# FiLM layer on one core: projections loaded as 16 partitions of four rows, contraction as four accumulated matmuls, compute in program order

## The chip, the cores and the metric

The kernel runs on one core of one Trainium2 chip. The metric is device time in microseconds (us). The times come on two levels: of the 29 runs of the kernel before in this study, 21 lie between 84.39 and 84.72 us and eight between 85.83 and 86.6. Runs more than 1.5% above the fastest of their kernel are marked slow.

## The reference, cut to what matters

```python
# x: (32, 512, 256) f32, conditioning: (32, 64), gamma_proj and beta_proj: (64, 256)
gamma = conditioning @ gamma_proj
beta = conditioning @ beta_proj
return x * (1 + gamma[:, None, :]) + beta[:, None, :]
```

A FiLM layer scales and shifts x by factors (gamma, beta) that a small input, the conditioning, sets. 16.78 MB come in, 16.78 MB go out, and each element gets one multiply and one add. The two small products (32 x 64 by 64 x 256) are all the arithmetic that TensorE has.

## The kernel before: the parts that the argument touches

x is treated as four slabs of eight batches; each slab gives every partition 32 rows of 256. All loads of x go out on SyncE's queue ahead of the compute (slab 0 in two parts, so five loads; four are issued in the first 3 us, the last at 10.3 us). The small inputs and all stores go out on ScalarE's queue. gamma and beta come out of TensorE already repeated onto the 128 partitions, because the conditioning matrix is transposed and repeated by a matmul against a repeated identity.

```python
nc.scalar.dma_start(out=cond_s, in_=conditioning)
gbproj = consts.tile([cond_dim, 2 * dim], f32)          # 64 partitions
nc.scalar.dma_start(out=gbproj[:, :dim], in_=gamma_proj)
nc.scalar.dma_start(out=gbproj[:, dim:], in_=beta_proj)
# ... loads of x on nc.sync, transposed and repeated conditioning in cond_T ...
for s in range(SLABS):
    nc.tensor.matmul(p_t, lhsT=cond_T[:, s * P : (s + 1) * P], rhs=gbproj, start=True, stop=True)
    nc.scalar.activation(out=s_t[:, :dim], in_=p_t[:, :dim], func=Identity, bias=1.0, scale=1.0)
    nc.scalar.copy(out=s_t[:, dim:], in_=p_t[:, dim:])
# ...
for s in range(SLABS):
    for r0 in range(0, ROWS, GROUP):                     # 2 pieces of 16 rows a slab
        # 11 rows on VectorE, 5 on GpSimd
        nc.vector.scalar_tensor_tensor(out=v, in0=rows(g_p, nv), scalar=1.0, in1=v, op0=ALU.add, op1=ALU.mult)
        nc.gpsimd.tensor_tensor(out=w, in0=w, in1=rows(g_s, nw), op=ALU.mult)
        nc.vector.tensor_add(out=v, in0=v, in1=rows(b_p, nv))
        nc.gpsimd.tensor_tensor(out=w, in0=w, in1=rows(b_s, nw), op=ALU.add)
        nc.scalar.dma_start(out=o_v[s, :, r0 : r0 + GROUP, :], in_=xs[:, r0 : r0 + GROUP, :])
```

Of the kernel before, what the change touches and what calls it, by code (L numbers as in the profile page):

```python
# [2 lines left out]

# [5 lines left out]


@with_exitstack
def kernel(
    ctx: ExitStack,
    tc: tile.TileContext,
    x: bass.AP,
    conditioning: bass.AP,
    gamma_proj: bass.AP,
    beta_proj: bass.AP,
    out: bass.AP,  # L20
):
    nc = tc.nc
    f32 = mybir.dt.float32
    ALU = mybir.AluOpType

    batch, seq, dim = x.shape
    cond_dim = conditioning.shape[1]
    P = 128
    SLABS = 4
    BS = batch // SLABS  # L30
    REP = P // BS
    ROWS = BS * seq // P
    assert SLABS * BS == batch and REP * BS == P and ROWS * REP == seq

    x_v = x.flatten_outer_dims().rearrange("(s p r) d -> s p r d", s=SLABS, p=P)
    o_v = out.flatten_outer_dims().rearrange("(s p r) d -> s p r d", s=SLABS, p=P)

    LOADS = {0: [8, 24]}
    GROUP = 16
    ON_DVE = 11  # L40

    consts = ctx.enter_context(tc.tile_pool(name="consts", bufs=1))
    xpool = ctx.enter_context(tc.tile_pool(name="xpool", bufs=1))
    psum = ctx.enter_context(tc.tile_pool(name="psum", bufs=1, space=bass.MemoryType.PSUM))


    cond_s = consts.tile([batch, cond_dim], f32)
    nc.scalar.dma_start(out=cond_s, in_=conditioning)  # L48
    gbproj = consts.tile([cond_dim, 2 * dim], f32)
    nc.scalar.dma_start(out=gbproj[:, :dim], in_=gamma_proj)  # L50
    nc.scalar.dma_start(out=gbproj[:, dim:], in_=beta_proj)

    slabs = []
    for s in range(SLABS):
        xs = xpool.tile([P, ROWS, dim], f32, name=f"xs{s}")
        slabs.append(xs)
        r = 0
        for n in LOADS.get(s, [ROWS]):
            nc.sync.dma_start(out=xs[:, r : r + n, :], in_=x_v[s, :, r : r + n, :])
            r += n  # L60
        assert r == ROWS


    ident = consts.tile([batch, batch], f32)
    make_identity(nc, ident)
    rident = consts.tile([batch, batch * REP], f32)
    nc.vector.tensor_copy(  # L67
        out=rident.rearrange("p (b g) -> p b g", g=REP),
        in_=ident.to_broadcast([batch, batch, REP]),
    )  # L70
    cond_T_p = psum.tile([cond_dim, batch * REP], f32)
    nc.tensor.matmul(cond_T_p, lhsT=cond_s, rhs=rident, start=True, stop=True)  # L72
    cond_T = consts.tile([cond_dim, batch * REP], f32)
    nc.vector.tensor_copy(out=cond_T, in_=cond_T_p)  # L74

    gb_p, gb_s = [], []
    for s in range(SLABS):
        p_t = psum.tile([P, 2 * dim], f32, name=f"gb_p{s}")
        nc.tensor.matmul(p_t, lhsT=cond_T[:, s * P : (s + 1) * P], rhs=gbproj,  # L79
                         start=True, stop=True)  # L80
        s_t = consts.tile([P, 2 * dim], f32, name=f"gb_s{s}")
        nc.scalar.activation(out=s_t[:, :dim], in_=p_t[:, :dim],  # L82
                             func=mybir.ActivationFunctionType.Identity,
                             bias=1.0, scale=1.0)
        nc.scalar.copy(out=s_t[:, dim:], in_=p_t[:, dim:])  # L85
        gb_p.append(p_t)
        gb_s.append(s_t)

    def rows(t, n):
        return bass.AP(tensor=t.tensor, offset=t.offset, ap=[t.ap[0], [0, n], t.ap[1]])  # L90

    for s in range(SLABS):
        xs = slabs[s]
        g_p, b_p = gb_p[s][:, :dim], gb_p[s][:, dim:]
        g_s, b_s = gb_s[s][:, :dim], gb_s[s][:, dim:]
        for r0 in range(0, ROWS, GROUP):
            v = xs[:, r0 : r0 + ON_DVE, :]
            w = xs[:, r0 + ON_DVE : r0 + GROUP, :]
            nv, nw = ON_DVE, GROUP - ON_DVE
            nc.vector.scalar_tensor_tensor(out=v, in0=rows(g_p, nv), scalar=1.0, in1=v,  # L100
                                           op0=ALU.add, op1=ALU.mult)
            nc.gpsimd.tensor_tensor(out=w, in0=w, in1=rows(g_s, nw), op=ALU.mult)  # L102
            nc.vector.tensor_add(out=v, in0=v, in1=rows(b_p, nv))  # L103
            nc.gpsimd.tensor_tensor(out=w, in0=w, in1=rows(b_s, nw), op=ALU.add)  # L104
            nc.scalar.dma_start(out=o_v[s, :, r0 : r0 + GROUP, :],
                                in_=xs[:, r0 : r0 + GROUP, :])


# [1 line left out]
_INS = ['x', 'conditioning', 'gamma_proj', 'beta_proj']  # L110
_OUTS = [((32, 512, 256), 'float32')]


# [23 lines left out]
```

## Time and profile before

| kernel before | |
|---|---|
| three runs | 84.39, 85.98, 85.95 us (median 85.95) |
| six runs, with three taken beside the changed kernel | median 84.53 us, four near 84.5, two near 86 |
| profiled run | 84.35 us, span 82.6 us |

The prediction below shows the lines that carry the bound. Two more groups help to read it: the elementwise work, and the small loads with their time from issue to landing (the moment when all of their data is reported in place). Columns of the first: line, engine, operation, tiles, shapes, count, then total busy us and mean ns of one, then the idle time before and what ended it.

```profile
L102 POOL TENSOR_TENSOR xs<-xs,gb_s 128x1280 f32<-128x1280 f32 x8 | 23.0, 2895 | 16.2 <-ACT gb_s L82 16.2
L100 DVE SCALAR_TENSOR_TENSOR xs<-gb_p,xs 128x2816 f32<-128x2816 f32 x8 | 24.7, 3083 | 10.9 <-ACT gb_s L85 10.9
...
gbproj<-in_gamma_proj_dram ACTq DMA_DIRECT2D x1, 64.0 KB, 9.1
gbproj<-in_beta_proj_dram ACTq DMA_DIRECT2D x1, 64.0 KB, 12.9
```

VectorE and GpSimd wait once, at the start, for the scaled gamma and beta. Those wait for 64 KB that take 12.9 us to arrive.

### The profile page before, as it was taken

How to read it: one execution, taken by the hardware profiler on the slowest of the kernel's cores; microseconds unless marked ns; L12 is line 12 of the kernel's file. 1: busy time of each engine (PE TensorE's matmuls, PEld its weight loads, DVE VectorE, ACT ScalarE, POOL GpSimd, SP SyncE). 2: the span in 40 equal slices, each digit the busy share in tenths (PEclk: the TensorE clock that was granted, in tenths of full speed). 3: DMA queues.
4: the chain of work that ended last, by engine and by line, in shares of the span. 5: the costliest groups of instructions: out<-in, count | busy, mean ns of one | idle time of the engine just before them, and what ended most of it. 6: DMA issues, size and time to landing. Idle time of an engine off the chain costs nothing.

```text
span 82.6 us, 156 instructions
## 1 busy us (share of the span) xinstructions
PE 9.1 (11%) x10; PEld 2.8 (3%) x10; DVE 49.9 (60%) x18; ACT 3.9 (5%) x9; POOL 46.2 (56%) x22
## 2 busy tenths in 40 slices
PE   0080000899600000000000000000000000000000
PEld 0100000443000000000000000000000000000000
DVE  2011000059999999999999999999999920000000
ACT  0600000034400000000000000000000000000000
POOL 2000000069999999999999999999995000000000
DMA  3899999969969989998889979899999999999992
GB/s 56 337 508 397 389 397 524 460 302 508 508 270 492 508 381 381 413 476 381 381 381 556 460 302 460 381 468 421 429 452 389 468 421 421 460 389 452 437 421 87
DMA packets 2080, 33.69 MB, mean 408 GB/s; under 512 B 288, under 2 KB 416, under 8 KB 416
## 3 DMA queue, kind: packets, MB, share of 16 engines
q1 hardware_dynamic: 720, 16.78, 48.6%
q10 hardware_dynamic: 1360, 16.92, 48.0%
HBM read 16.92 MB, written 16.78 MB: 408 GB/s over the span
## 4 chain that ended last, share of the span: by engine, by line
DVE 49%; DMA 16%; issue 11%; PE 2%; ACTq 1%; ACT 1%
DVE xs L100 30%; DVE xs L103 19%; DMA gbproj<-in_beta_proj_dram 16%; PE gb_p L79 2%; ACTq L50 1%; ACTq L48 0%; ACT gb_s L82 0%; ACT gb_s L85 0%
## 5 line engine op out<-in xcount | busy, mean ns | idle before, releaser
L102 POOL TENSOR_TENSOR xs<-xs,gb_s 128x1280 f32<-128x1280 f32 x8 | 23.0, 2895 | 16.2 <-ACT gb_s L82 16.2
L100 DVE SCALAR_TENSOR_TENSOR xs<-gb_p,xs 128x2816 f32<-128x2816 f32 x8 | 24.7, 3083 | 10.9 <-ACT gb_s L85 10.9
L103 DVE TENSOR_TENSOR xs<-xs,gb_p 128x2816 f32<-128x2816 f32 x8 | 24.7, 3086 | 0.3
L104 POOL TENSOR_TENSOR xs<-xs,gb_s 128x1280 f32<-128x1280 f32 x8 | 23.0, 2893 | 0.0
L79 PE MATMUL gb_p<-gbproj,cond_T 64*128 64x512 f32 x8 | 7.2, 1074 | 8.9 <-DMA gbproj<-in_beta_proj_dram 8.9
L74 DVE COPY cond_T<-cond_T_p 64x512 f32<-64x512 f32 x1 | 0.7, 683 | 4.3 <-PE cond_T_p L72 4.3
L79 PEld LDWEIGHTS gb_p<-gbproj,cond_T 64*128 64x128 f32 x8 | 2.5, 328 | 13.7 <-issue 13.7
L72 PE MATMUL cond_T_p<-rident,cond_s 32*64 32x512 f32 x2 | 1.9, 1065 | 3.9 <-DMA cond_s<-in_conditioning_dram 3.9
L82 ACT ACTIVATE gb_s<-gb_p 128x256 f32<-128x256 f32 x4 | 1.5, 383 | 16.4 <-PE gb_p L79 16.4
L85 ACT COPY gb_s<-gb_p 128x256 f32<-128x256 f32 x4 | 1.5, 367 | 0.0
L82 ACT ACT_TABLE_LOAD x1 | 1.3, 1283 | 2.4 <-issue 2.4
L67 DVE COPY rident<-ident 32x512 f32<-32x512 f32 x1 | 0.4, 416 | 1.2 <-POOL ident masks.py:199 1.2
L72 PEld LDWEIGHTS cond_T_p<-rident,cond_s 32*64 32x64 f32 x2 | 0.3, 202 | 3.9 <-issue 3.9
masks.py:197 POOL MEMSET ident<- 32x32 f32 x1 | 0.1, 114 | 0.3 <-POOLq L121 0.3
masks.py:199 POOL TENSOR_SCALAR_AFFINE_SELECT ident<-ident 32x32 f32<-32x32 f32 x1 | 0.2, 202 | 0.1
L121 POOL MEMSET const-float32-0.0<- 128x1 f32 x1 | 0.1, 103 | 0.2 <-issue 0.2
L121 POOL MEMSET const-bfloat16-1.0<- 128x1 bf16 x1 | 0.1, 106 | 0.0
L121 POOL MEMSET const-uint8-127<- 128x1 uint8 x1 | 0.1, 106 | 0.0
L121 POOL MEMSET const-float32-1.0<- 128x1 f32 x1 | 0.1, 103 | 0.0
## 6 DMA issues: line engine op xcount, KB each, us to landing
out_dram<-xs ACTq DMA_DIRECT2D x8, 2048.0 KB, 18.2
xs<-in_x_dram SPq DMA_DIRECT2D x3, 4096.0 KB, 32.9
xs<-in_x_dram SPq DMA_DIRECT2D x1, 3072.0 KB, 12.2
xs<-in_x_dram SPq DMA_DIRECT2D x1, 1024.0 KB, 4.6
gbproj<-in_gamma_proj_dram ACTq DMA_DIRECT2D x1, 64.0 KB, 9.1
gbproj<-in_beta_proj_dram ACTq DMA_DIRECT2D x1, 64.0 KB, 12.9
cond_s<-in_conditioning_dram ACTq DMA_DIRECT2D x1, 8.0 KB, 3.0
```

Of the source, the lines that this page charges most:

```text
L50: nc.scalar.dma_start(out=gbproj[:, :dim], in_=gamma_proj)
L67: nc.vector.tensor_copy(out=rident.rearrange("p (b g) -> p b g", g=REP), in_=ident.to_broadcast([batch, batch, REP]),)
L72: nc.tensor.matmul(cond_T_p, lhsT=cond_s, rhs=rident, start=True, stop=True)
L74: nc.vector.tensor_copy(out=cond_T, in_=cond_T_p)
L79: nc.tensor.matmul(p_t, lhsT=cond_T[:, s * P : (s + 1) * P], rhs=gbproj, start=True, stop=True)
L82: nc.scalar.activation(out=s_t[:, :dim], in_=p_t[:, :dim], func=mybir.ActivationFunctionType.Identity, bias=1.0, scale=1.0)
L85: nc.scalar.copy(out=s_t[:, dim:], in_=p_t[:, dim:])
L100: nc.vector.scalar_tensor_tensor(out=v, in0=rows(g_p, nv), scalar=1.0, in1=v, op0=ALU.add, op1=ALU.mult)
L102: nc.gpsimd.tensor_tensor(out=w, in0=w, in1=rows(g_s, nw), op=ALU.mult)
L103: nc.vector.tensor_add(out=v, in0=v, in1=rows(b_p, nv))
L104: nc.gpsimd.tensor_tensor(out=w, in0=w, in1=rows(b_s, nw), op=ALU.add)
L121: nc = _bacc.Bacc("TRN2", target_bir_lowering=False, num_devices=1)
```

## The change

The intent is to start computing earlier. The projections take longest among the inputs of the first piece (12.9 us from issue to landing for beta_proj, 12.2 for rows 8 to 31 of slab 0), so they are laid out as 16 partitions of four rows: one run of 4 KB a partition, 16 packets a projection instead of 64. (A packet is one entry of the trace's list of DMA work. Here a data packet is one contiguous run, and the page counts the packets' time as a share of the time of 16 DMA engines. In the packet records before, gamma_proj's 64 packets of 1 KB start in four rounds of 16, 0.95 us apart.) The contraction over 64 is then four accumulated matmuls of 16. The elementwise work is fixed in program order, with GpSimd alternating multiply and add.

```diff
-    gbproj = consts.tile([cond_dim, 2 * dim], f32)
-    nc.scalar.dma_start(out=gbproj[:, :dim], in_=gamma_proj)
-    nc.scalar.dma_start(out=gbproj[:, dim:], in_=beta_proj)
+    CP = 16
+    CJ = cond_dim // CP
+    gproj = consts.tile([CP, CJ, dim], f32)
+    bproj = consts.tile([CP, CJ, dim], f32)
+    gproj_src = gamma_proj.rearrange("(q j) d -> q j d", j=CJ)
+    bproj_src = beta_proj.rearrange("(q j) d -> q j d", j=CJ)
     # ... the same five x loads on nc.sync, in program order now between the small loads ...
+    nc.scalar.dma_start(out=gproj, in_=gproj_src)
+    nc.scalar.dma_start(out=bproj, in_=bproj_src)
     # ... cond_T_p by 4 small matmuls, one repeated copy c_t for each slab ...
-        nc.tensor.matmul(p_t, lhsT=cond_T[:, s * P : (s + 1) * P], rhs=gbproj, start=True, stop=True)
+        for half, proj in ((p_t[:, :dim], gproj), (p_t[:, dim:], bproj)):
+            for j in range(CJ):
+                nc.tensor.matmul(half, lhsT=c_t[:, j, :], rhs=proj[:, j, :], start=j == 0, stop=j == CJ - 1)
     # ...
-    for s in range(SLABS):
+    with tc.manual_schedule():
+        for s, sl in enumerate(slabs):
             # same pieces, same 11 / 5 split, same stores on nc.scalar
```

More of the change, by code (lines that the diff above doesn't have):

```diff
@@ L28 @@
     P = 128
-    SLABS = 4
-    BS = batch // SLABS
-    REP = P // BS
-    ROWS = BS * seq // P
-    assert SLABS * BS == batch and REP * BS == P and ROWS * REP == seq
-    x_v = x.flatten_outer_dims().rearrange("(s p r) d -> s p r d", s=SLABS, p=P)
-    o_v = out.flatten_outer_dims().rearrange("(s p r) d -> s p r d", s=SLABS, p=P)
-    LOADS = {0: [8, 24]}
-    GROUP = 16
-    ON_DVE = 11
+    SLABS = [(8, [8, 24]), (8, [32]), (8, [32]), (8, [32])]
+    assert sum(n for n, _ in SLABS) == batch
+    STORES = [[16, 16], [16, 16], [16, 16], [16, 16]]
+    PIECE, ON_DVE = 16, 11
+    x_f = x.flatten_outer_dims()
+    o_f = out.flatten_outer_dims()
     consts = ctx.enter_context(tc.tile_pool(name="consts", bufs=1))
@@ L44 @@
     psum = ctx.enter_context(tc.tile_pool(name="psum", bufs=1, space=bass.MemoryType.PSUM))
-    cond_s = consts.tile([batch, cond_dim], f32)
-    nc.scalar.dma_start(out=cond_s, in_=conditioning)
-    gbproj = consts.tile([cond_dim, 2 * dim], f32)
-    nc.scalar.dma_start(out=gbproj[:, :dim], in_=gamma_proj)
-    nc.scalar.dma_start(out=gbproj[:, dim:], in_=beta_proj)
-    slabs = []
-    for s in range(SLABS):
-        xs = xpool.tile([P, ROWS, dim], f32, name=f"xs{s}")
-        slabs.append(xs)
-        r = 0
-        for n in LOADS.get(s, [ROWS]):
-            nc.sync.dma_start(out=xs[:, r : r + n, :], in_=x_v[s, :, r : r + n, :])
-            r += n
-        assert r == ROWS
+    slabs = []
@@ new lines, with load @@
+    b0 = 0
+    for s, (n, loads) in enumerate(SLABS):
+        assert P % n == 0
+        rows = n * seq // P
+        r0, r1 = b0 * seq, (b0 + n) * seq
+        slabs.append(dict(
+            n=n, b0=b0, rows=rows, loads=loads,
+            src=x_f[r0:r1, :].rearrange("(p r) d -> p r d", p=P),
+            dst=o_f[r0:r1, :].rearrange("(p r) d -> p r d", p=P),
+            xs=xpool.tile([P, rows, dim], f32, name=f"xs{s}"),
+        ))
+        b0 += n
+    def load(eng, s, i):
+        sl = slabs[s]
+        r = sum(sl["loads"][:i])
+        n = sl["loads"][i]
+        eng.dma_start(out=sl["xs"][:, r : r + n, :], in_=sl["src"][:, r : r + n, :])
@@ new lines @@
+    CP = 16
+    CJ = cond_dim // CP
+    cond_s = consts.tile([batch, cond_dim], f32)
+    gproj = consts.tile([CP, CJ, dim], f32)
+    bproj = consts.tile([CP, CJ, dim], f32)
+    gproj_src = gamma_proj.rearrange("(q j) d -> q j d", j=CJ)
+    bproj_src = beta_proj.rearrange("(q j) d -> q j d", j=CJ)
+    load(nc.sync, 0, 0)
+    nc.scalar.dma_start(out=cond_s, in_=conditioning)
+    load(nc.sync, 0, 1)
+    nc.scalar.dma_start(out=gproj, in_=gproj_src)
+    load(nc.sync, 1, 0)
+    nc.scalar.dma_start(out=bproj, in_=bproj_src)
@@ L64 @@
+    load(nc.sync, 2, 0)
+    load(nc.sync, 3, 0)
     ident = consts.tile([batch, batch], f32)
     make_identity(nc, ident)
-    rident = consts.tile([batch, batch * REP], f32)
-    nc.vector.tensor_copy(
-        out=rident.rearrange("p (b g) -> p b g", g=REP),
-        in_=ident.to_broadcast([batch, batch, REP]),
-    )
-    cond_T_p = psum.tile([cond_dim, batch * REP], f32)
-    nc.tensor.matmul(cond_T_p, lhsT=cond_s, rhs=rident, start=True, stop=True)
-    cond_T = consts.tile([cond_dim, batch * REP], f32)
@@ L74 @@
-    nc.vector.tensor_copy(out=cond_T, in_=cond_T_p)
-    gb_p, gb_s = [], []
-    for s in range(SLABS):
+    gb_p, gb_s = [], []
+    cond_T_p = psum.tile([CP, CJ, batch], f32)
+    for j in range(CJ):
+        nc.tensor.matmul(cond_T_p[:, j, :],
+                         lhsT=cond_s.rearrange("b (q j) -> b j q", j=CJ)[:, j, :],
+                         rhs=ident, start=True, stop=True)
+    for s, sl in enumerate(slabs):
+        n, b0 = sl["n"], sl["b0"]
+        rep = P // n
+        c_t = consts.tile([CP, CJ, P], f32, name=f"cond_T{s}")
+        nc.vector.tensor_copy(
+            out=c_t.rearrange("q j (b g) -> q j b g", g=rep),
+            in_=cond_T_p[:, :, b0 : b0 + n].to_broadcast([CP, CJ, n, rep]),
+        )
@@ L78 @@
         p_t = psum.tile([P, 2 * dim], f32, name=f"gb_p{s}")
-        nc.tensor.matmul(p_t, lhsT=cond_T[:, s * P : (s + 1) * P], rhs=gbproj,
-                         start=True, stop=True)
+        for half, proj in ((p_t[:, :dim], gproj), (p_t[:, dim:], bproj)):
+            for j in range(CJ):
+                nc.tensor.matmul(half, lhsT=c_t[:, j, :], rhs=proj[:, j, :],
+                                 start=j == 0, stop=j == CJ - 1)
         s_t = consts.tile([P, 2 * dim], f32, name=f"gb_s{s}")
@@ L87, with spread @@
         gb_s.append(s_t)
-    def rows(t, n):
+    def spread(t, n):
         return bass.AP(tensor=t.tensor, offset=t.offset, ap=[t.ap[0], [0, n], t.ap[1]])
-    for s in range(SLABS):
-        xs = slabs[s]
-        g_p, b_p = gb_p[s][:, :dim], gb_p[s][:, dim:]
-        g_s, b_s = gb_s[s][:, :dim], gb_s[s][:, dim:]
-        for r0 in range(0, ROWS, GROUP):
-            v = xs[:, r0 : r0 + ON_DVE, :]
-            w = xs[:, r0 + ON_DVE : r0 + GROUP, :]
-            nv, nw = ON_DVE, GROUP - ON_DVE
-            nc.vector.scalar_tensor_tensor(out=v, in0=rows(g_p, nv), scalar=1.0, in1=v,
-                                           op0=ALU.add, op1=ALU.mult)
-            nc.gpsimd.tensor_tensor(out=w, in0=w, in1=rows(g_s, nw), op=ALU.mult)
-            nc.vector.tensor_add(out=v, in0=v, in1=rows(b_p, nv))
-            nc.gpsimd.tensor_tensor(out=w, in0=w, in1=rows(b_s, nw), op=ALU.add)
-            nc.scalar.dma_start(out=o_v[s, :, r0 : r0 + GROUP, :],
-                                in_=xs[:, r0 : r0 + GROUP, :])
+    with tc.manual_schedule():
+        for s, sl in enumerate(slabs):
+            xs = sl["xs"]
+            g_p, b_p = gb_p[s][:, :dim], gb_p[s][:, dim:]
+            g_s, b_s = gb_s[s][:, :dim], gb_s[s][:, dim:]
+            done = 0
+            for n in STORES[s]:
+                for q0 in range(done, done + n, PIECE):
+                    nv, nw = ON_DVE, PIECE - ON_DVE
+                    v = xs[:, q0 : q0 + nv, :]
+                    w = xs[:, q0 + nv : q0 + PIECE, :]
+                    nc.vector.scalar_tensor_tensor(out=v, in0=spread(g_p, nv), scalar=1.0, in1=v,
+                                                   op0=ALU.add, op1=ALU.mult)
+                    nc.gpsimd.tensor_tensor(out=w, in0=w, in1=spread(g_s, nw), op=ALU.mult)
+                    nc.vector.tensor_add(out=v, in0=v, in1=spread(b_p, nv))
+                    nc.gpsimd.tensor_tensor(out=w, in0=w, in1=spread(b_s, nw), op=ALU.add)
+                nc.scalar.dma_start(out=sl["dst"][:, done : done + n, :],
+                                    in_=xs[:, done : done + n, :])
+                done += n
+            assert done == sl["rows"]
 _INS = ['x', 'conditioning', 'gamma_proj', 'beta_proj']
```

## The prediction

> **What bounds the kernel now.** I read the page from the top, then the chain of waits, the windows by stage, the timeline of the first 30 us, and the packet records of the trace. First the busy shares, the row of the DMA engines and the queues:
>
> ```profile
> span 82.6 us, 156 instructions
> PE 9.1 (11%) x10; PEld 2.8 (3%) x10; DVE 49.9 (60%) x18; ACT 3.9 (5%) x9; POOL 46.2 (56%) x22
> ...
> DMA  3899999969969989998889979899999999999992
> GB/s 56 337 508 397 389 397 524 460 302 508 508 270 492 508 381 381 413 476 381 381 381 556 460 302 460 381 468 421 429 452 389 468 421 421 460 389 452 437 421 87
> ...
> q1 hardware_dynamic: 720, 16.78, 48.6%
> q10 hardware_dynamic: 1360, 16.92, 48.0%
> ```
>
> No compute engine passes 60%, but the two DMA queues together fill 48.6 + 48.0 = 96.6% of the time of the 16 engines. q1 holds the loads of x, q10 the small inputs and the stores. The dips in the DMA row come from slicing: a long packet is booked in the slice where it sits. In the packet records the first packet starts at 1.7 us and the last ends at 81.4 us; the packets' own times, summed over all queues and divided by 16, give 79.76 us for these 79.65 us. There is no hole. Wide windows agree:
>
> ```profile
> 44.00:48.00 4.00, 0.00 (x0) 0.00 (x0) 3.96 (x2) 0.00 (x0) 4.00 (x2) 1.00 0.91 393
> 48.00:52.00 4.00, 0.00 (x0) 0.00 (x0) 3.96 (x3) 0.00 (x0) 4.00 (x3) 1.00 0.99 422
> ...
> 68.00:72.00 4.00, 0.00 (x0) 0.00 (x0) 0.00 (x0) 0.00 (x0) 0.00 (x0) 1.00 0.98 418
> 72.00:76.00 4.00, 0.00 (x0) 0.00 (x0) 0.00 (x0) 0.00 (x0) 0.00 (x0) 1.00 1.02 438
> 76.00:80.00 4.00, 0.00 (x0) 0.00 (x0) 0.00 (x0) 0.00 (x0) 0.00 (x0) 1.00 1.00 430
> ```
>
> The last two columns are the DMA share and GB/s. VectorE (third pair) is finished at 66.6 us and the DMA engines run 15 us more at an unchanged rate. So the kernel is bound by its bytes: 33.69 MB in 79.65 us, 423 GB/s.
>
> The chain of waits tells a different story, and has to be read with care:
>
> ```profile
> DVE xs L100 30%; DVE xs L103 19%; DMA gbproj<-in_beta_proj_dram 16%; PE gb_p L79 2%; ACTq L50 1%; ACTq L48 0%; ACT gb_s L82 0%; ACT gb_s L85 0%
> ```
>
> It charges 16% to the load of beta_proj and 49% to VectorE, because it follows the issue of the last store back. But that store waits behind older stores already queued, so making its issue earlier does not by itself make its end earlier. This is the whole question of the change, which attacks exactly that 16%:
>
> ```profile
> 1.72 0.61 ACTq L51 DMA_DIRECT2D gbproj<-in_beta_proj_dram  x1
> 14.76 7.16 PE L79 MATMUL gb_p<-gbproj,cond_T 64*128 64x512 f32 x8 [8.90 <-DMA gbproj<-in_beta_proj_dram]
> 17.30 5.76 POOL L102 TENSOR_TENSOR xs<-xs,gb_s 128x1280 f32<-128x1280 f32 x2 [16.18 <-ACT gb_s L82]
> 17.52 3.09 DVE L100 SCALAR_TENSOR_TENSOR xs<-gb_p,xs 128x2816 f32<-128x2816 f32 x1 [10.94 <-ACT gb_s L85]
> 25.94 4.32 ACTq L105 DMA_DIRECT2D out_dram<-xs  x2
> ```
>
> beta_proj is issued at 1.72 us, lands at 14.6, and the first elementwise work starts at 17.5 us.
>
> [...]after the engines have started on gamma_proj, its 1 KB packets (46 ns each) appear once per 0.95 us, one per 24 KB packet of x (0.92 us). [...]The trace has only 512 columns (two passes per fp32 matmul, starts 0.85 us apart); I use the proportion as an estimate for 256.
>
> **The change part by part.**
>
> (1) Projection loads. Before, 64 rows of 1 KB give each of 16 engines 4 packets, then a semaphore packet, for each of gamma and beta: 5 turns apiece. After, 16 rows of 4 KB give 1 packet plus the semaphore: 2 turns. Gamma's first packet came at 5.6 us; I keep that. One turn of 0.95 us gives landing at about 6.7 us (was 10.3). Beta then takes two turns more: about 8.8 us instead of 14.6. The load itself is shortened by nearly 6 us.
>
> (2) TensorE. Instead of 4 matmuls of 512 columns (8 passes, 7.16 us busy) there are 32 of 256 columns (64 passes). At half of 0.85, or 0.43 us a pass, one slab's group costs 16 x 0.43 = 6.8 us against 1.7 us before, and all four 27 us. The weight load of 0.33 us stays under the 0.43. Group 0: gamma half from 6.7 to 10.2, beta half to 13.7 us (it is then bound by TensorE, not by beta's landing). ScalarE's two copies cost 0.38 + 0.27 as before: 14.3 us. So most of what (1) wins is paid back here; 3.1 us remain, first VectorE work at about 14.4 instead of 17.5 us. The other load needed, rows 8 to 31 of slab 0, landed at 13.4 us and should come near 13.1, so it does not decide. Later groups finish at about 20.5, 27.3 and 34.2 us; their slabs want them at 26.7, 39 and 51 us, so VectorE never waits.
>
> (3) Preparation. The 0.42 us copy of the identity goes; one 0.68 us copy of cond_T becomes four of the same free size, of which the first alone is needed before group 0, at about 5 us. All beside the wait for gamma: 0 us.
>
> (4) Program order. Listing the instructions by engine shows the same VectorE and GpSimd work (8 + 8 and 8 + 8 of the same sizes, 49.4 and 46 us), GpSimd now alternating multiply and add instead of doing two of each. The surprise is ScalarE's queue: the first store stands behind the copies for slab 2, the second behind those for slab 3. The piece would be ready at about 20.6 us, but the store goes out near 28 us (before: 25.9), the second near 35 us (before: about 30). By part (2) stores start later although compute starts earlier. The loads bridge this: 16.8 MB alone need some 39 us, and they are in flight from 1.7 us on.
>
> (5) Sum on the DMA engines. Bytes are the same. 128 packets of 1 KB become 32 of 4 KB: per engine 8 x 46 ns = 0.37 us against 2 x 0.153 = 0.31 us (4 KB at the 26.8 GB/s of the large packets), 0.06 us; with the six fewer turns at most 0.2 us. VectorE ends at about 63.5 instead of 66.6 us, and its last stores join a queue that has 15 to 18 us of work. Net: span about 82.4 us, time about 84.2 us in the state of the profiled run (84.35).
>
> **Rivals.** (a) Everything on the 16% is real, and the end comes 3 us sooner (81.3 us, 4%). For it: the chain. Against: it needs 33.69 MB in 76.5 us, 440 GB/s, while the best long stretch of the packet records holds 433. Rejected. (b) TensorE or ScalarE's in-order queue becomes the bound. If a pass of 256 columns cost the 1.07 us mean of a 512 one, 64 passes would take 68 us, slab 3 could not start before 75 us, and the end would be near 95 us. Against: starts were 0.85 us apart with 512 columns streaming back to back. Unlikely, 3%. (c) The DMA engines run dry between the last load and the stores. Loads alone to 32 us at 424 GB/s leave 4 MB, which at the two-thirds share they got beside stores before (about 300 of 433 GB/s) end near 46 us; by then about five pieces of 2 MB are computed, and at most one and a half are stored. No hole. (d) Packets slow down where stores begin: 391 to 419 GB/s from 28 to 33 us, some 0.4 us. This moves but stays.
>
> **Range and chances.** Before has two levels: 84.35 and 84.39, and 85.95 and 85.98, 1.9% apart; nothing in this profile explains the upper one. I expect 84.2 on the lower level and 85.8 on the upper, each about as likely as the median of a few runs. I name 85.0 between them; 83.6 to 86.2 holds both. On the same level the difference is -0.2%: within 2% by 0.83. Faster 0.13, mostly for a comparison of medians across levels, or an effect of the order on the upper level. Slower 0.04, for (b).
>
> **What would show it.** Right: DMA queues still near 97%; beta landing near 9 us; first VectorE work at 13 to 15 us and its last near 63.5; TensorE 25 to 35 us busy; first store issued near 28 us; a tail of pure stores of about 18 us instead of 15. Wrong: passes of 256 columns at about 1 us spacing, a VectorE wait for a matmul in mid-kernel, a DMA hole near 46 us, or a sustained rate above 440 GB/s.

The sum came to a span of about 82.4 us and a time of about 84.2 us. A turn in step (1) is the pace of small packets in this trace: gamma_proj's rounds of 1 KB packets start at 5.61, 6.56, 7.51 and 8.48 us, 0.95 to 0.97 us apart. The 0.43 us for a pass of 256 columns in step (2) is the author's estimate, half of the 0.85 us measured with 512 columns (the "proportion" of the text: half the columns, half the time); no trace showed it before the change was run.

## The result, and the profile after

| | median, us | runs | fast runs over fast runs of before |
|---|---|---|---|
| before | 84.53 | 84.39 to 85.98 (6, two slow) | |
| after | 84.59 | 84.48 to 87.71 (6, one slow) | 1.0014, 95% interval 0.9996 to 1.0032 |

Here and below a ratio is the recorded one, of fast runs over fast runs of the same rounds, so it is not quite the ratio of the medians quoted. The result is: the same, within 0.3%. The profiled run is fast, 84.62 us.

First the page of the changed kernel: span, busy shares, DMA row, queues and chain.

```profile
span 82.9 us, 281 instructions
PE 28.2 (34%) x72; PEld 21.5 (26%) x72; DVE 51.3 (62%) x20; ACT 3.9 (5%) x9; POOL 46.5 (56%) x22
...
DMA  1897999999899699999999899999999999999991
...
q1 hardware_dynamic: 720, 16.78, 48.5%
q10 hardware_dynamic: 1264, 16.92, 47.8%
...
DVE xs L126 29%; DVE xs L129 19%; PE gb_p L102 9%; DMA gproj<-in_gamma_proj_dram 8%; ACTq L74 0%; ACT gb_s L105 0%; ACT gb_s L108 0%
```

The 16% that the chain charged to the load of beta_proj has become 8% for gamma_proj and 9% for TensorE. Yet the two DMA queues still fill 96.3% of the 16 engines' time, and the span has not moved. Then the timeline of the start (start, duration, engine, line, operation; in brackets the idle time before):

```profile
1.17 0.44 ACTq L76 DMA_DIRECT2D gproj<-in_gamma_proj_dram  x1
8.24 3.75 PE L102 MATMUL gb_p<-gproj,cond_T 16*128 16x256 f32 x8 [3.47 <-DMA gproj<-in_gamma_proj_dram]
11.78 3.62 PE L102 MATMUL gb_p<-bproj,cond_T 16*128 16x256 f32 x8
16.12 3.09 DVE L126 SCALAR_TENSOR_TENSOR xs<-gb_p,xs 128x2816 f32<-128x2816 f32 x1 [8.83 <-ACT gb_s L108]
29.09 0.38 ACT L105 ACTIVATE gb_s<-gb_p 128x256 f32<-128x256 f32 x1 [6.18 <-PE gb_p L102]
29.23 0.38 ACTq L131 DMA_DIRECT2D out_dram<-xs  x1
```

gamma_proj is in TensorE's hands at 8.2 us. The beta half follows with no idle time in brackets: beta_proj had landed by then (8.9 us after its issue at 1.64, so 10.5). The first VectorE work starts at 16.1 us, 1.4 us earlier than the 17.5 before. The first store goes out at 29.2 us, right behind slab 2's scaling in ScalarE's queue, 3.3 us later than before. And the tail, in the windows by stage (the last two columns are the DMA share and GB/s):

```profile
64.00:68.00 4.00, 0.00 (x0) 0.00 (x0) 1.19 (x1) 0.00 (x0) 0.00 (x0) 1.00 1.00 426
68.00:72.00 4.00, 0.00 (x0) 0.00 (x0) 0.00 (x0) 0.00 (x0) 0.00 (x0) 1.00 1.00 430
72.00:76.00 4.00, 0.00 (x0) 0.00 (x0) 0.00 (x0) 0.00 (x0) 0.00 (x0) 1.00 1.02 438
76.00:80.00 4.00, 0.00 (x0) 0.00 (x0) 0.00 (x0) 0.00 (x0) 0.00 (x0) 1.00 0.98 418
```

VectorE stops at 65.2 us (before: 66.6). The last packet ends at 81.7 us (before: 81.4). The 1.4 us gained at the start lie in a longer queue of stores.

**A measure for small effects.** The trace holds a record of each packet, with start, size and own time; these records are not on the page. The figures below come from one profiled run of each kernel. Undisturbed packets of x take 309, 912 and 1213 ns for 8, 24 and 32 KB. I call surplus what x packets took beyond that, summed and divided by 16 engines:

| surplus, us per engine | 8 KB | 24 KB | 32 KB | all |
|---|---|---|---|---|
| before | 0.45 | 0.20 | 0.57 | 1.22 |
| after | 0.41 | 0.83 | 0.00 | 1.24 |

Two effects of about 0.6 us cancel. In the changed kernel, the x packets that run beside the 4 KB packets of the projections take 1.30 to 1.36 us (medians) instead of 0.91. Of the 0.57 us before, 0.11 lie beside beta_proj's packets, and 0.46 between 28 and 33 us, around the first stores; the changed kernel has none of the latter.

### The profile page after: what moved, and what is told of

The parts are those of the page before. It is cut to its first block, busy times and chain, and to the rows that moved or that the text cites. A ratio compares the mean times of both kernels' runs of the same rounds, so it can differ in the third digit from the quotient of the medians.

```text
span 82.9 us, 281 instructions
## 1 busy us (share of the span) xinstructions
PE 28.2 (34%) x72; PEld 21.5 (26%) x72; DVE 51.3 (62%) x20; ACT 3.9 (5%) x9; POOL 46.5 (56%) x22
## 2 busy tenths in 40 slices
DMA packets 1984, 33.69 MB, mean 407 GB/s; under 512 B 288, under 2 KB 288, under 8 KB 320
## 4 chain that ended last, share of the span: by engine, by line
DVE 48%; issue 11%; PE 9%; DMA 8%; ACT 1%; ACTq 0%
DVE xs L126 29%; DVE xs L129 19%; PE gb_p L102 9%; DMA gproj<-in_gamma_proj_dram 8%; ACTq L74 0%; ACT gb_s L105 0%; ACT gb_s L108 0%
## 5 line engine op out<-in xcount | busy, mean ns | idle before, releaser
L102 PE MATMUL gb_p<-gproj,cond_T 16*128 16x256 f32 x32 | 14.6, 633 | 3.5 <-DMA gproj<-in_gamma_proj_dram 3.5
L102 PE MATMUL gb_p<-bproj,cond_T 16*128 16x256 f32 x32 | 14.5, 629 | 0.0
L102 PEld LDWEIGHTS gb_p<-gproj,cond_T 16*128 16x128 f32 x32 | 10.5, 330 | 6.4 <-DVE cond_T L95 3.6
L102 PEld LDWEIGHTS gb_p<-bproj,cond_T 16*128 16x128 f32 x32 | 10.6, 332 | 3.0
L95 DVE COPY cond_T<-cond_T_p 16x512 f32<-16x512 f32 x4 | 2.5, 672 | 4.8 <-PE cond_T_p L88 4.8
L88 PE MATMUL cond_T_p<-ident,cond_s 32*16 32x32 f32 x8 | 0.6, 232 | 4.2 <-DMA cond_s<-in_conditioning_dram 4.2
```

Source lines behind the costliest of these rows:

```text
L88: nc.tensor.matmul(cond_T_p[:, j, :], lhsT=cond_s.rearrange("b (q j) -> b j q", j=CJ)[:, j, :], rhs=ident, start=True, stop=True)
L95: nc.vector.tensor_copy(out=c_t.rearrange("q j (b g) -> q j b g", g=rep), in_=cond_T_p[:, :, b0 : b0 + n].to_broadcast([CP, CJ, n, rep]),)
L102: nc.tensor.matmul(half, lhsT=c_t[:, j, :], rhs=proj[:, j, :], start=j == 0, stop=j == CJ - 1)
```

## The experiments

My theory: the bytes on the 16 DMA engines set the end, and the time at which compute starts has slack. Rivals: the chain of waits is real and something in the change gives the gain back (its program order, TensorE, or slower loads). Eleven kernels were run, all with correct output; "before" was timed beside each.

### e1: more bytes

One more load of 2.1 MB into a tile that nothing reads, added to the changed kernel.

```diff
+    extra = xpool.tile([P, 16, dim], f32, name="extra")
+    nc.sync.dma_start(out=extra, in_=slabs[0]["src"][:, :16, :])
```

> The changed kernel with one more load of 2.1 MB into a tile that nothing reads, queued behind the last load of x. If the bytes on the DMA engines set the end, the time grows by 2.1 MB / 0.431 MB per us = 4.9 us, to about 89.4 us (ratio to before 1.058), with VectorE still ending near 65 us. If the chain of VectorE work and the last store's issue set the end, the last store's way stays the same and the time grows by less than 1 us.

Measured: 89.71 us median, fast runs 89.67 to 89.72 and one slow of 91.9, 5.1 us above the changed kernel's 84.59. In the packet records first packet to last packet takes 84.84 us instead of 79.93: 4.91 us, the predicted 4.9. VectorE's last instruction, at line 131 here, is where it was:

```profile
span 87.9 us, 281 instructions
...
L131 DVE TENSOR_TENSOR xs<-xs,gb_p x8: 3086/3087/3089, 19.2 to 62.0; 128x2816 f32<-128x2816 f32 x8
```

It starts at 62.0 us (62.1 in the changed kernel), so compute did not move and the end did. The chain theory fails. (e1 to e4 were timed beside the same seven runs of before, of which four were slow. The record's ratios for these four have wide intervals, here 1.0549, 1.041 to 1.0688, and the verdict "unclear"; they cannot come from the three runs marked fast alone, whose mean is 84.58. Over that mean, e1's fast runs give 1.061. For e1 to e4 I therefore compare times with those three, 84.49 to 84.65.)

### e2 and e3: beta_proj later on purpose

The opposite of the change, on the kernel before: the load of beta_proj goes behind a large load on the same queue. Both have program order, which e8 tests by itself.

```diff
-    nc.scalar.dma_start(out=gbproj[:, dim:], in_=beta_proj)
     # in the loop of the x loads
+        if s == 1:            # e3: s == 2
+            nc.sync.dma_start(out=gbproj[:, dim:], in_=beta_proj)
```

> The kernel before, in program order, with the load of beta_proj put behind slab 1's load on the same queue, so that it lands near 21 to 23 us instead of 14.6. First VectorE work near 24 us instead of 17.5, last near 73 instead of 66.6. DMA theory: the backlog of stores covers it and the time stays at 84.5 us (ratio 1.00). Rival, the chain: 6.5 us more, about 91 us (1.077).

> The same with beta_proj behind slab 2's load: landing near 31 us, first VectorE work near 34 us, last near 83 us, past the old end. DMA theory: the backlog is used up, a hole opens near 41 to 46 us and before each late store, and the time becomes compute end plus one store, about 83 + 7 + 1.5 = 91 us (1.08). The chain alone: 16.5 us more, 101 us (1.195).

Measured: e2 84.47 us (four runs, all fast, 84.34 to 84.58; 0.999 of the fast mean of before), e3 94.1 us (all fast, 94.07 to 94.23; 1.113). The lines of the first multiply, e2 then e3 (after the count: shortest, median and longest ns, then first and last start in us):

```profile
L102 DVE SCALAR_TENSOR_TENSOR xs<-gb_p,xs x8: 3083/3084/3091, 26.4 to 69.2; 128x2816 f32<-128x2816 f32 x8
```

```profile
L102 DVE SCALAR_TENSOR_TENSOR xs<-gb_p,xs x8: 3083/3084/3092, 36.0 to 78.9; 128x2816 f32<-128x2816 f32 x8
```

Starting compute 8.9 us later (26.4 against 17.5; I had expected 24) costs nothing. In e2 the DMA engines are as full as ever while VectorE works late:

```profile
64.00:68.00 4.00, 0.00 (x0) 0.00 (x0) 3.97 (x2) 0.00 (x0) 3.94 (x2) 1.00 1.00 430
72.00:76.00 4.00, 0.00 (x0) 0.00 (x0) 3.40 (x2) 0.00 (x0) 0.77 (x1) 1.00 1.00 430
```

Starting it 18.5 us later costs 9.6 us (94.1 against 84.5). So the kernel before had about 9 us of slack there, and an earlier start adds to slack that is already unused. The packet records agree: per engine, e2 has 79.66 us of packets between first and last packet, 79.65 us apart, and e3 has 80.80 us of them in 89.36 us, a hole of 8.6 us in all. In both, the last packet ends 6.0 us after VectorE; so e2 uses up the slack almost exactly. e3 came 3 us above my 91: beta_proj landed later than I had put it, and VectorE started at 36.0 instead of 34. Its windows show how a missed slack looks, with DMA engines waiting for compute:

```profile
64.00:68.00 4.00, 0.00 (x0) 0.00 (x0) 4.00 (x2) 0.00 (x0) 3.92 (x3) 1.00 0.77 328
72.00:76.00 4.00, 0.00 (x0) 0.00 (x0) 3.97 (x3) 0.00 (x0) 3.92 (x2) 1.00 0.70 299
76.00:80.00 4.00, 0.00 (x0) 0.00 (x0) 4.00 (x2) 0.00 (x0) 3.92 (x3) 1.00 0.71 303
```

The same stretches of the kernel before have a DMA share of 1.00 to 1.06.

### e4: everything of the change but the layout

64 partitions of one row, so one matmul of 256 columns for each half; issue order and program order of the change kept.

```diff
-    CP = 16
+    CP = 64
```

> The changed kernel with 64 partitions of one row for the projections (1 KB runs, one matmul of 256 columns each instead of four): program order and issue order of the change alone, without its layout. beta_proj lands again near 14 us, TensorE is busy under 9 us, the first store leaves near 24 us instead of 29. DMA theory: 84.5 us (ratio within 0.5% of 1). Chain: first VectorE work near 17, so about 1 us slower than the changed kernel. Small x packets: the surplus of the 24 KB packets of x over their median should fall from 0.83 us per DMA engine (changed kernel) back to about 0.1 (before).

Measured: 84.40 us, three runs from 84.37 to 84.42 and a fourth of 85.59, which lies just inside the 1.5% and counts as fast (ratio 0.996, interval 0.9813 to 1.0108; verdict unclear, as said under e1). TensorE was busy 7.9 us, the first store left at 23.2 us, six us before that of the changed kernel, and nothing came of it. Surplus of the 24 KB packets: 0.23 us (expected: 0.1; the kernel before has 0.20), so the slow x packets go with the layout.

### e5 and e6: what slows the packets of x, the run or the partitions

e5 keeps 16 partitions but gives each four separate rows, so runs of 1 KB. e6 takes 32 partitions with runs of 2 KB.

```diff
     # e5 (same for bproj_src), with the matching rearrangement of cond_s
-    gproj_src = gamma_proj.rearrange("(q j) d -> q j d", j=CJ)
+    gproj_src = gamma_proj.rearrange("(j q) d -> q j d", j=CJ)
     # e6
-    CP = 16
+    CP = 32
```

> The changed kernel with row q + 16 j in place of row 4 q + j on partition q: still 16 partitions and four accumulated matmuls, but runs of 1 KB, so 4 packets a DMA engine and projection as before the change. Time: 84.5 us, within 0.5%. For the slowed 24 KB packets of x (surplus 0.83 us per DMA engine in the changed kernel, 0.1 to 0.2 with 64 partitions): if it is the 16 partitions that do it[...], the surplus stays above 0.4; if it is the 4 KB run, it falls under 0.25. beta_proj lands near 14 us.

(The clause cut from e5's expectation guessed at why 16 partitions would slow the packets; no run shows that.)

> The changed kernel with 32 partitions of two rows (2 KB runs, two matmuls): surplus of the 24 KB packets between 0.15 and 0.45 us per DMA engine under both readings; under the partitions reading nearer 0.2. beta_proj lands near 10.5 to 11 us, TensorE busy about 14 us, first VectorE work set by rows 8 to 31 of slab 0 (13.1 to 14 us), the earliest of all. Time by the DMA theory 84.5 us, within 0.5%; by the chain 2 us less than the changed kernel.

| | partitions, run | surplus of 24 KB packets, us | median, us | ratio to before |
|---|---|---|---|---|
| after | 16, 4 KB | 0.83 | 84.59 | 1.0014 (0.9996 to 1.0032) |
| e5 | 16, 1 KB | 1.00 (and 0.28 of 32 KB) | 85.03 | 1.0043 (1.0014 to 1.0073) |
| e6 | 32, 2 KB | 0.19 | 84.57 | 0.9988 (0.997 to 1.0007) |
| e4 | 64, 1 KB | 0.23 | 84.40 | 0.996 (0.9813 to 1.0108) |

e5 has the run length of the kernel before and a larger surplus still: it is the partitions, not the run. Its time shows it, 0.4% over before, and 0.6% over the 84.5 us that I had expected within 0.5%. beta_proj landed at 15.8 us there (expected: 14; in the kernel before 14.6): the x packets beside the small ones took some 1.0 to 1.1 us each instead of 0.91, over eight turns. e6 had the early start at 14.4 us that the change was after (beta_proj landed at 11.5 us, TensorE was busy 14.7 us), and no gain in time.

### e7 and e8: program order undone, and alone

```diff
     # e7, changed kernel                 # e8, kernel before
-    with tc.manual_schedule():          +    order = ctx.enter_context(tc.manual_schedule())
+    if True:                            (ahead of the compute loop)
```

> The changed kernel without its program order: GpSimd does two multiplies, then two adds, as in the kernel before; everything else is kept. DMA theory: 84.5 us, within 0.5%. A theory in which the program order offsets a gain of the layout: faster than the changed kernel by 1 us or more.

> The kernel before with program order alone (GpSimd alternates multiply and add), the layout of the projections untouched. First store leaves near 23.7 us instead of 25.9. DMA theory: 84.5 us, within 0.5%. It also shows whether the upper level of 85.8 to 86.6 us, which the kernel before shows in about half of its runs and the others in one of seven, goes with its order of instructions: if so this kernel shows it rarely, and e7 often.

Measured: e7 84.61 us (ratio 0.9989, interval 0.9969 to 1.0008), e8 84.64 us (0.9997, 0.9981 to 1.0014). In e8 the first store left at 24.1 us instead of 25.9; no effect. Program order neither gives nor takes.

e7's profiled run happened to be a slow one (87.27 us), so it shows where the slow level lost its time in this one run. Its windows, before and after the first stores' packets, which start at 33 us:

```profile
16.00:20.00 4.00, 4.00 (x11) 3.09 (x10) 3.84 (x2) 0.09 (x1) 4.00 (x2) 1.00 1.02 393
20.00:24.00 4.00, 4.00 (x11) 3.15 (x10) 4.00 (x2) 0.65 (x2) 4.00 (x2) 1.00 1.02 393
24.00:28.00 4.00, 4.00 (x10) 3.06 (x10) 3.96 (x2) 0.00 (x0) 4.00 (x3) 1.00 1.02 393
44.00:48.00 4.00, 0.00 (x0) 0.00 (x0) 4.00 (x2) 0.00 (x0) 4.00 (x3) 1.00 1.03 442
```

In the packet records x comes in at 387 GB/s from 8 to 30 us after the first packet, against 433 in the fast run of the changed kernel. A 32 KB packet takes 1356 ns (median) instead of 1213. From the first stores on, the rate is the usual 433. So 22 us at 387 instead of 433 cost 22 x (1 - 387 / 433) = 2.3 us. The surplus of all x packets is 3.94 us against 1.24 in the changed kernel's fast run; these 2.7 us are the whole difference in time. e7, which shares the order of the elementwise work with the kernel before, was slow in one of five runs, e8 in none of four, before in eight of the 29 runs, four of them in one session. So I can't say that the slow level goes with anything in the change; what causes it stays open.

### e9 and e10: neighbouring or spread partitions, measured by themselves

One extra load of 0.52 MB on 16 partitions, eight runs of 4 KB each, added to e4. The two kernels differ in one subscript.

```diff
+    junk_src = x_f[:1024, :].rearrange("(q k a r) d -> q k a (r d)", q=16, k=8, a=2)
+    nc.scalar.dma_start(out=junk[0:16, :, :], in_=junk_src[:, :, 0, :])       # e9
+    nc.scalar.dma_start(out=junk[0:128:8, :, :], in_=junk_src[:, :, 0, :])    # e10
```

> The kernel of e4 (64 partitions for the projections) with one extra load of 0.52 MB into a tile that nothing reads: 16 neighbouring partitions, eight runs of 4 KB each, so 8 packets on each of the 16 DMA engines, issued after beta_proj. Its bytes alone cost 0.52 / 0.431 = 1.2 us (85.7 us). If neighbouring partitions are what slows the x packets, each of the 8 turns costs some 0.4 us as the two turns of the changed kernel did: 3 us more, about 88 to 89 us. If it was the run length alone, the same 3 us appear in e10 too.

> The same extra load with the 16 partitions taken eight apart (0, 8, .. 120), same bytes, same 4 KB runs, same queue. If neighbouring partitions are the cause: about 85.7 to 86.2 us, x packets hardly slowed. If the run length is the cause: as e9.

Measured: e9 90.2 us (ratio 1.0671, interval 1.064 to 1.0703; expected 88 to 89), e10 87.34 us (1.0329, 1.0291 to 1.0367). Same bytes, same runs, same queue: the neighbouring partitions cost 2.9 us more. Windows while the extra load was moving, e9 then e10:

```profile
16.00:20.00 4.00, 4.00 (x11) 3.09 (x10) 3.05 (x1) 1.61 (x6) 3.19 (x2) 1.00 1.00 311
20.00:24.00 4.00, 1.35 (x4) 0.53 (x2) 3.97 (x3) 0.98 (x4) 4.00 (x2) 1.00 0.96 294
24.00:28.00 4.00, 0.00 (x0) 0.00 (x0) 3.96 (x2) 0.00 (x0) 3.92 (x2) 1.00 1.06 286
```

```profile
16.00:20.00 4.00, 4.00 (x10) 3.12 (x10) 3.26 (x2) 1.85 (x6) 3.43 (x2) 1.00 0.86 317
20.00:24.00 4.00, 1.11 (x3) 0.33 (x1) 4.00 (x2) 0.74 (x3) 4.00 (x2) 1.00 1.14 412
24.00:28.00 4.00, 0.00 (x0) 0.00 (x0) 3.97 (x2) 0.00 (x0) 3.92 (x2) 1.00 0.87 311
```

The twelve microseconds average 297 GB/s in e9 and 347 in e10. Surplus of the 32 KB packets: 4.16 us against 1.86 us (0.54 in e4). With the extra packets' own time, 1.81 and 1.52 us per engine, that accounts for 5.4 of the 5.8 us by which e9 lies above e4, and for 2.8 of the 2.9 us of e10. So e10 is not free either, and my 85.7 to 86.2 for it was too low. The large surpluses are those of 16 neighbouring partitions: 0.83 us (after) and 1.00 us (e5) on the 24 KB packets, 4.16 us (e9) on the 32 KB packets. The same 16 taken eight apart slowed the x packets less (1.86 us), and projections on 32 or 64 partitions left 0.19 and 0.23 us. The runs show that the time depends on the partitions; what carries it is not shown here.

### e11: a try at a faster version

32 partitions as in e6, and the stores of slabs 1 and 2 as one of 4 MB each.

```diff
-    CP = 16
+    CP = 32
-    STORES = [[16, 16], [16, 16], [16, 16], [16, 16]]
+    STORES = [[16, 16], [32], [32], [16, 16]]
```

> A try at the best: 32 partitions for the projections (e6) and the stores of slabs 1 and 2 as one of 4 MB each, so that half of the store packets are 32 KB. A 16 KB store packet took 611 ns, a 32 KB load packet 1213 ns against 2 x 611: 512 x 9 ns / 2 / 16 = 0.15 us less. DMA theory: 84.3 to 84.5 us, 0.997 to 1.0 of before, within the noise. Any gain over 1% would contradict it.

Measured: 84.41 us, five fast runs from 84.29 to 84.43, ratio 0.998 (0.9966 to 0.9994). The 0.2% by which it lies below before is of the size of the packet sum, which said 0.15 us less. No order of work tried here gives more. The engines are full from 1.7 to 81.4 us; 33.69 MB at the 433 GB/s of an undisturbed stretch are 77.8 us, so by this estimate some 1.8 us at most could come from smoother packets.

## Why the prediction was right or wrong, point by point

- **The bound.** Right: a kernel of DMA bytes, with the chain's 16% not on offer. e1 (4.91 us for 2.1 MB), e2 (8.9 us of delay for nothing) and e3 (18.5 us for 9.6) show it. Rival (a), 81.3 us, fell.
- **Range and chances: the step that failed.** The mechanism was right, and a size was wrong. The working gave 84.2 us and -0.2% on one level, and I then named 85.0, half-way between the two levels, because of three runs of before two were high. Beside a median of 85.95 that 85.0 stood for a gain of 1.1% that no step of the working had produced. In the next three runs before was at 84.44 to 84.54 each time, its median of six is 84.53, and the changed kernel's 84.59: +0.14% on the fast runs. A value between two levels belongs to neither; the number should have been the fast level's 84.2, with the upper level only in the range. In the sum itself the mis-sized term is the turn of step (1): 0.95 us kept, 1.5 us measured. The x packets that it slowed took 0.63 us more where step (5) had said up to 0.2 us less in all. The range was too narrow for single runs as well: a slow run of the changed kernel took 87.71 us. The changed kernel's median lies inside it.
- **Step (1), projection loads.** Mis-sized: gamma_proj landed at 8.1 us instead of 6.7, beta_proj at 10.5 instead of 8.8. Two things were wrong. I kept 0.95 us for a turn, and the turn beside gamma's 4 KB packets took 1.5 us (first data packet at 5.69 us, first 4-byte semaphore packet at 7.15), because the x packets took 1.30 to 1.36 us in place of 0.91, which I had not foreseen. And I took one turn after the first packet for the landing: in the trace the last engine's semaphore packet comes 0.5 us after the first one's (7.67 us), and the load lands 0.44 us after that. The kernel before shows the same two (0.31 and 0.46 us), so 6.7 us was too early already by the trace that it was read from.
- **Step (2), TensorE.** Right: 16 passes (records of the trace, two for each fp32 matmul here) from 8.24 to 15.41 us, 0.43 us apart, 28.2 us busy in all. Halving the 0.85 us of 512 columns was right. The whole chain came 1.7 us late, 1.4 of it by gamma's landing: first VectorE work at 16.1 us, not 14.4, last at 65.2, not 63.5. Rival (b) fell; no wait for a matmul in mid-kernel.
- **Step (3), preparation.** Right: the four copies of 0.67 us lay beside the wait for gamma_proj.
- **Step (4), ScalarE's queue.** Right: first store at 29.2 us (said: near 28) and the second at 36.0 (near 35), held behind the scaling of slabs 2 and 3. That this costs nothing is shown by e4 and e8, whose first stores leave at 23.2 and 24.1 us.
- **Step (5), the sum.** Up to 0.2 us less was said; the packet records give 1.22 us of surplus before and 1.24 after. The projections' own packets shrank only from 0.37 to 0.35 us, and the slowed 24 KB packets of x took 0.63 us more. That the 32 KB packets took 0.57 us less and made up for it was not foreseen; that the sum came out level is in part luck.
- **Rival (c).** No hole between loads and stores, as said. **(d)** was said to move but stay; in the changed kernel the slow packets around the first stores are gone (0.00 against 0.46 us). e4, e6, e8 and e11 have them too (0.44 to 0.53 us), e1 almost not and e5 not. Why is open.

## What to carry to other kernels

Before speeding up what the chain of waits charges, ask whether the shared engine behind it is full. Here the DMA queues added up to 96.6% of the span, and to all of the time from first to last packet: a start 1.4 us earlier only lengthened the queue (ratio 1.0014), and a delay put in on purpose (e2, 8.9 us at 0.999) showed the slack in one run. Look also at what a small load does to the loads beside it: laid out on 16 neighbouring partitions, the projections landed earlier but gave the 24 KB packets of x a surplus of 0.83 us; on 32 the surplus was 0.19 us and compute started earliest, at 14.4 us. When times come on two levels, predict one level and put the other in the range.
